# A weight stream whose two parts are made by the loads themselves: a rounding transfer and an adding one

## The chip, the cores and the metric

The kernel runs on one core of a Trainium2 chip. The metric is the device time of one execution in microseconds, the median of three runs; lower is better.

## The reference

Two layers of an encoder over 512 tokens of 1024 features, all in float32. Each layer projects the normed input, mixes it in three branches, merges them by gates, and adds a gated feed-forward part and an embedding part:

```python
for i in range(DEPTH):                       # DEPTH = 2
    z = rmsnorm(x, mix_norm[i]) @ w_in[i]    # 1024 x 6312
    u_rnn, u_gelu, c_q, ckv_rope, fq, fk, fv, f_logit, gate_logit = split_columns(z)
    y_a = rglru_branch(u_rnn, u_gelu, ...) @ w_br_a[i]
    y_b = mla_branch(c_q, ckv_rope, ...) @ w_br_b[i]
    y_c = fox_branch(fq, fk, fv, f_logit, fox_bf[i]) @ w_br_c[i]
    g = sigmoid(gate_logit + gate_b[i]).reshape(B, S, 3, D)
    x = x + (g[:, :, 0] * y_a + g[:, :, 1] * y_b + g[:, :, 2] * y_c) @ w_o[i]
    hf = rmsnorm(x, ffn_norm[i]) @ w_gate_up[i]
    x = x + (silu(hf[..., :D_FF]) * hf[..., D_FF:]) @ w_down[i]      # D_FF = 2816
    x = x + sigmoid(rmsnorm(x, ple_norm[i]) @ w_ple_gate[i]) * (p[i] @ w_ple[i])
return rmsnorm(x, final_norm)
```

What matters here is the number of weights: about 40 million float32 values, each used once for all 512 tokens.

## The kernel before

Activations lie feature by token, in pages of 128 features by 512 tokens. TensorE multiplies float32r values; to keep float32 accuracy, each operand X is held as two float32r parts, hi (X rounded) and lo (X minus hi), and each product is three matmuls, hi by hi, hi by lo and lo by hi (`mm3`). So each 128x128 weight tile costs three matmuls of 512 columns.

The weights come as one stream in the order of use (class `Stream`). A unit is four tiles side by side, 128 partitions by 512 columns, 256 KB; there are 606 of them (`NUNITS`). Before, a unit passes through two rings. `_load` (L99) brings it by a transfer on SP's queue into one of four pages of the tile `raw`. `_split` makes the two parts in one of five pages of `hl`, each of 512 columns of hi and 512 of lo: ScalarE casts raw into hi (L112), VectorE subtracts hi from raw into lo (L113). `_ensure`, called when the first tile of a unit is taken, records loads and splits ahead of the products, as far as the rings reach. The last 16 units (from `KEPT` on) get pages of the large pool `pr` in place of pages of `hl`, since they are used twice, each time for half the tokens. Four units (`PACKED`) have both parts side by side for a narrow product.

Other names that matter: `pf` and `pr` are pools of pages (float32, and float32r with both parts), `bank` the eight PSUM banks. L221, L218, L225 are VectorE helpers, L230 and L233 ScalarE helpers, L237 is every matmul. POOL issues small transfers beside its memsets: masks and rotary tables (L403, L404, L493), a row's copies for attention (L587, L592, L594, L937), the input of the residual (L1010), the embedding input (L1083), and x between the layers (L1113).

The order on each engine is set by a scheduler, which goes by data dependence and simulated readiness; what stands in `high_priority()` goes first among what is ready. Every engine then runs its own queue in order, and an instruction that waits for a semaphore holds back all that is behind it. POOL's transfers count on eight semaphores in turn (DMASW0 to DMASW7 in the orders below), so each also waits for the transfer issued eight before it.

Of the kernel before, what the change touches and what calls it, by code (L numbers as in the profile page):

```python
# [26 lines left out]
# columns of w_in  # L27
# [3 lines left out]
# columns of the small per-partition vectors, per layer  # L31
# [3 lines left out]
V_LAM = DEPTH * NV          # lambdas of all layers, side by side  # L35
# [3 lines left out]
NUNITS = 606                # units of four 128x128 weight tiles in the stream  # L39
KEPT = NUNITS - 16          # from here on the stream is kept on chip: it is used twice  # L40
PACKED = (8, 9, 311, 312)  # units whose tiles hold the parts of 64 columns side by side


class Pages:
    """Pages of one tile, handed out oldest-freed first."""
# [39 lines left out]
class Stream:  # L85
    """The weights, in the order in which TensorE uses them: loaded ahead, split into two
    float32r parts that sum to the float32 value."""

    def __init__(self, tc, wdram, raw, hl, nraw, nhl):
        self.tc, self.nc, self.wdram, self.raw, self.hl = tc, tc.nc, wdram, raw, hl  # L90
        self.nraw, self.nhl = nraw, nhl
        self.pos, self.spec = 0, []
        self.loaded, self.done = 0, 0
        self.pages, self.kept = None, {}

    def _load(self, u):
        s = (u % self.nraw) * 512
        c = 512 * (u % 2)
        self.nc.sync.dma_start(self.raw[:, s:s + 512], self.wdram[u // 2][:, c:c + 512])  # L99

    def _split(self, u):
        s = (u % self.nraw) * 512
        src = self.raw[:, s:s + 512]
# [7 lines left out]
        with self.tc.high_priority():  # L111
            self.nc.scalar.copy(hi, src)  # L112
            self.nc.vector.tensor_tensor(lo, src, hi.bitcast(F32), op=ALU.subtract)  # L113
# [8 lines left out]
    def _ensure(self, u):  # L122
        last = min(u + self.nhl - 1, NUNITS - 1)
        while self.loaded < min(self.nraw, NUNITS):
            self._load(self.loaded)
            self.loaded += 1
        while self.done <= last:
            self._split(self.done)
            self.done += 1
            while self.loaded < min(self.done + self.nraw, NUNITS):  # L130
                self._load(self.loaded)
                self.loaded += 1

    def tile(self, spec):
        """hi and lo of the next 128x128 tile"""
# [7 lines left out]
    def again(self, i):  # L143
        """tile i of the stream, one of those that were kept"""
# [7 lines left out]
    def wide(self, spec):  # L152
        """hi and lo of a 128x512 tile, at the start of a unit"""
# [13 lines left out]
class Trunk:  # L167
    def __init__(self, ctx, tc, wst, vec, xT, pT, trig, masks, outT, last):
# [7 lines left out]
        NR, NF, NRAW, NHL = 31, 20, 4, 5  # L176
# [26 lines left out]
    # -- small things ---------------------------------------------------------------------  # L203

    def cols(self, n):
        """n columns of a ring of small per-partition values"""
# [37 lines left out]
    # -- products, as generators that stop after every k tile -----------------------------  # L244

    def dense(self, spec, xs, evac, m=128):
        """out[m, tokens] = sum over k of W[k, m] * X[k, tokens]; xs are pages"""
# [11 lines left out]
    def group(self, specs, xs, evacs):  # L259
        """several of them side by side, k tile by k tile"""  # L260
# [20 lines left out]
    # -- RMSNorm ---------------------------------------------------------------------------  # L281

    def norm_add(self, st, x):
        """adds the squares of x (128 features) to the sums of norm st"""
# [17 lines left out]
    def norm_sum(self, st, n, fold=None):  # L302
        """token-major 1/rms, times fold, and its diagonal for the broadcast"""
# [10 lines left out]
        # 1/sqrt(v): a first value from the bits of v, good to 2e-3, and three Newton steps  # L314
# [30 lines left out]
    def normed(self, x, g):  # L345
        """page with both parts of x * g"""
# [5 lines left out]
    def after_norm(self, st, n, gen, s1, s2):  # L352
        """the first products after a norm, whose results wait for it; the sums are taken after
        s1 of their steps and the broadcast after s2"""
# [11 lines left out]
    # -- set-up -----------------------------------------------------------------------------  # L366

    def log1p_exp_neg(self, out, t1, t2, u, e):
        """out = log1p(s) / 2 with s = exp(-|u|), as atanh(y) with y = s / (2 + s)"""
# [11 lines left out]
    def setup(self):  # L381
# [6 lines left out]
        for k in range(KD):  # L388
            nc.sync.dma_start(self.x[k].ap, self.a_x[k])
            if k < 4:  # L390
                self.w._load(k)
        self.w.loaded = 4
        # TensorE's clock rises while it is busy
# [30 lines left out]
        # softplus(-lambda), times 2  # L424
# [9 lines left out]
    # -- mixers -------------------------------------------------------------------------------  # L434
# [4 lines left out]
    def mix(self, layer):  # L439
# [6 lines left out]
        # recurrent branch  # L446
# [39 lines left out]
        # rotary key and forget logits  # L486
# [12 lines left out]
        def rope(z, src, out_h, out_l, m):  # L499
            """z may be src"""  # L500
# [8 lines left out]
        def key_and_forget():  # L509
            """the rotary key, and the sums of the log forget gates; both parts of the weights side  # L510
            by side, so that one pass serves both"""
# [33 lines left out]
        # attention pieces  # L545
        qp, kp = {}, {}

        def ev_heads(pages, p, r, fox, is_q):
            """two heads' queries or keys to their pages, times 1/rms unless r is None"""
            f8 = 0.125 if fox and is_q else 1.0  # L550

            def f(b):
# [21 lines left out]
                for e in range(2):  # L574
# [3 lines left out]
                    if fox:  # L578
                        # queries [hi, hi | lo, extra], keys [hi, lo | hi, extra] or [lo, hi | hi, extra]
# [26 lines left out]
        def values(spec, X, rT):  # L606
            """token-major values: page per token tile, [head][hi 64 | lo 64]"""
# [23 lines left out]
        # recurrence: gates, then the scan  # L631
# [32 lines left out]
        def lru_tail():  # L664
            # one change of ScalarE's tables for all of them
# [724 lines left out]
```

## Time and profile before

| | |
|---|---|
| runs | 1825.26 us median (1824.38, 1825.26, 1826.84) |
| profiled execution, first to last instruction | 1825.0 us (no other time of it is given) |
| granted TensorE clock, mean | 0.996 |
| HBM read, written | 173.98 MB, 4.21 MB, 98 GB/s over the span |
| weight loads on SP's queue | 606 of 256 KB, 2.6 us from issue to landing |

In the rows below, a group of instructions reads: line, engine, operation, output<-inputs, count | busy us in total, mean ns of one | idle us of its engine just before them, and what ended most of that idle time. A row of waits reads: engine and line that waited <- what it waited for: us in total, times, longest. A row of the timeline reads: start us, duration us, engine, line, operation, count, and the idle time before it in brackets. A row of stretches reads: from:to, length, busy us of the asked instructions (their count), granted clock, share of the DMA engines busy, GB/s. A row of a DMA queue reads: packets, MB, share of 16 engines' span; one of DMA issues ends in KB and the median us from issue to landing.

### The profile page before, as it was taken

To read this page: it belongs to the slowest core of one execution; us is meant where nothing else is said; L and a number is where in the kernel's file an instruction comes from. 1 tells how busy PE (TensorE), PEld (TensorE's weight loads), DVE (VectorE), ACT (ScalarE), POOL (GpSimd) and SP (SyncE) were. 2 spreads that over 40 slices of the span, in tenths; PEclk is the share of its full clock that TensorE was granted. 3 is DMA by queue.
4 is the path that set the end of the run, shared out by engine and by line. 5 is a ranking of instruction groups with operands and counts; after the bars stand their busy time and mean duration, and the time that the engine had idled before them with its cause. 6 is when DMAs were issued, how large, how long until landed. Compare 5 with 4: busy or idle time off the path is not lost. (4 is left out here: it accounts for less than half of the span.)

```text
span 1825.0 us, 24155 instructions
## 1 busy us (share of the span) xinstructions
PE 1807.5 (99%) x8490; PEld 1505.6 (82%) x8490; DVE 1210.6 (66%) x2421; ACT 817.1 (45%) x1562; POOL 117.2 (6%) x234
## 2 busy tenths in 40 slices
PE   9999999999999999999999999999999999999998
PEld 8778888888888888888887788888888888888887
DVE  8997678866665555444778966888576555553457
ACT  4766556553333333223447655565533333332243
POOL 1220001100000000000103200010000000000000
PEclk9999999999999999999999999999999999999999
DMA  5232223324222222322333322242232222232231
GB/s 178 91 131 82 81 78 117 97 72 139 96 95 96 96 98 98 110 94 97 133 110 122 106 81 82 91 116 85 87 128 92 99 98 97 95 109 99 98 116 47
DMA packets 98826, 184.17 MB, mean 101 GB/s; under 512 B 13552, under 2 KB 14752, under 8 KB 98704
## 3 DMA queue, kind: packets, MB, share of 16 engines
q1 hardware_dynamic: 89280, 162.04, 25.7%
q0 software_dynamic: 8416, 19.45, 3.8%
q8 instruction: 66, 1.08, 0.2%
q10 hardware_dynamic: 1008, 1.14, 0.2%
q14 instruction: 56, 0.46, 0.1%
HBM read 173.98 MB, written 4.21 MB: 98 GB/s over the span
## 5 line engine op out<-in xcount | busy, mean ns | idle before, releaser
L237 PE MATMUL bank<-pr,hl 128*128 128x512 f32 (+1 forms) x6812 | 1602.9, 392 | 2.8 <-ACT pr L233 1.1
L237 PEld LDWEIGHTS bank<-pr,hl 128*128 128x128 f32 (+1 forms) x6812 | 1269.9, 188 | 267.3 <-ACT pr L233 2.0
L112 ACT CAST hl<-raw 128x512 fp32r<-128x512 f32 x590 | 364.3, 618 | 672.0 <-PE bank L237 403.8
L113 DVE TENSOR_TENSOR hl<-raw,hl 128x512 fp32r<-128x512 f32 x590 | 404.2, 686 | 378.6 <-ACT hl L112 360.4
L221 DVE TENSOR_TENSOR pf<-pf 128x512 f32<-128x512 f32 (+3 forms) x235 | 151.1, 651 | 31.8 <-ACT pf L230 29.9
L221 DVE TENSOR_TENSOR pf<-bank,pf 128x512 f32<-128x512 f32 (+3 forms) x198 | 132.8, 676 | 58.6 <-PE bank L237 32.1
L230 ACT ACTIVATE pf<-pf 128x512 f32<-128x512 f32 (+1 forms) x145 | 86.1, 600 | 112.7 <-DVE pf L221 110.5
L237 PE MATMUL bank<-pr 128*128 128x256 f32 (+5 forms) x704 | 120.7, 303 | 4.1 <-ACT pf L230 2.2
L237 PEld LDWEIGHTS bank<-pr 128*128 128x128 f32 (+1 forms) x704 | 102.7, 191 | 14.1 <-ACT pf L230 2.7
L221 DVE TENSOR_TENSOR pr<-pf,pr 128x512 fp32r<-128x512 f32 (+2 forms) x126 | 85.6, 682 | 4.5 <-ACT pr L233 3.5
L230 ACT ACTIVATE pf<-bank,small 128x384 f32<-128x384 f32 (+3 forms) x130 | 68.9, 531 | 38.5 <-DVE small L836 35.4
L233 ACT CAST pr<-pf 128x512 fp32r<-128x512 f32 (+1 forms) x114 | 70.4, 620 | 33.2 <-DVE pf L218 23.1
L853 ACT CAST pth<-bank 128x128 fp32r<-128x128 f32 (+3 forms) x128 | 54.0, 427 | 58.7 <-PE bank L828 50.5
L221 DVE TENSOR_TENSOR ptl<-bank,pth 128x128 fp32r<-128x128 f32 (+3 forms) x128 | 61.7, 485 | 13.9 <-ACT pth L853 9.9
L836 DVE TENSOR_REDUCE small<-bank 128x1 f32<-128x384 f32 (+3 forms) x128 | 61.6, 484 | 7.6 <-PE bank L237 6.5
L237 PE MATMUL bank<-hl,pr 128*128 128x512 f32 x240 | 56.3, 391 | 0.4 <-DVE hl L113 0.4
L828 PE MATMUL bank<-identr,pf 128*128 128x128 f32 x320 | 55.0, 273 | 0.0
L237 PEld LDWEIGHTS bank<-hl,pr 128*128 128x128 f32 x240 | 44.7, 188 | 10.3 <-DVE hl L113 1.1
L225 DVE TENSOR_SCALAR pf<-pf,small 128x384 f32<-128x384 f32 (+3 forms) x128 | 48.6, 383 | 2.6
L828 PEld LDWEIGHTS bank<-identr,pf 128*128 128x128 f32 x320 | 40.2, 140 | 8.3
L218 DVE SCALAR_TENSOR_TENSOR pf<-pf,bank 128x512 f32<-128x512 f32 x48 | 32.6, 683 | 21.6 <-PE bank L237 21.2
L230 ACT ACTIVATE pf<-bank,vec 128x512 f32<-128x512 f32 x60 | 40.9, 689 | 12.9 <-PE bank L237 12.5
(112 smaller groups left out, 796.6 us busy)
## 6 DMA issues: line engine op xcount, KB each, us to landing
raw<-wst SPq DMA_DIRECT2D x606, 256.0 KB, 2.6
pf<-xT POOLq DMA_DIRECT2D x16, 256.0 KB, 3.3
pr<-pr POOLq DMA_DIRECT2D x32, 128.0 KB, 2.6
pf<-xs POOLq DMA_DIRECT2D x16, 256.0 KB, 3.2
pf<-trig POOLq DMA_DIRECT2D x12, 256.0 KB, 3.1
pf<-xT SPq DMA_DIRECT2D x8, 256.0 KB, 5.3
xs<-pf POOLq DMA_DIRECT2D x8, 256.0 KB, 2.7
pf<-pT POOLq DMA_DIRECT2D x4, 256.0 KB, 3.1
```

Source lines behind the costliest of these rows:

```text
L112: self.nc.scalar.copy(hi, src)
L113: self.nc.vector.tensor_tensor(lo, src, hi.bitcast(F32), op=ALU.subtract)
L218: self.nc.vector.scalar_tensor_tensor(out, a, s, b, op0=op0, op1=op1)
L221: self.nc.vector.tensor_tensor(out, a, b, op=op)
L225: self.nc.vector.tensor_scalar(out, a, s1, None, op0=op0)
L230: return self.nc.scalar.activation(out, a, f, **kw)
L233: self.nc.scalar.copy(hi, src)
L237: self.nc.tensor.matmul(out, a, b, start=start, stop=stop, skip_group_check=True)
L828: nc.tensor.transpose(T[:, c], p2.ap[:, c], self.ident[:, :])
L836: nc.vector.reduce_max(R[t][:, 0:1], S[:, :m], axis=AX.X, negate=True)
L853: self.nc.scalar.copy(hi, src)
```

## The change

`raw` is no longer used for weights. For each unit POOL issues a transfer from HBM into hi that casts float32 to float32r; ScalarE writes the negative of hi into lo; POOL issues a second transfer of the same 256 KB from HBM that adds the weights onto lo. VectorE takes no part. `_load` and `_split` become one function, `hl` has six pages where it had five, and `raw` has two where it had four (its later use as scratch pages, near the end, has two as well). Comments are taken out elsewhere, which moves the line numbers: L112 and L113 have their counterparts in L109 (rounding transfer), L110 (negation) and L111 (adding transfer); L237 becomes L228, L221 L212, L230 L221, L233 L224, L493 L481, L1083 L1071.

```diff
     def _load(self, u):
-        s = (u % self.nraw) * 512
         c = 512 * (u % 2)
-        self.nc.sync.dma_start(self.raw[:, s:s + 512], self.wdram[u // 2][:, c:c + 512])
-
-    def _split(self, u):
-        s = (u % self.nraw) * 512
-        src = self.raw[:, s:s + 512]
+        src = self.wdram[u // 2][:, c:c + 512]
         if u >= KEPT:
             self.kept[u] = self.pages.take()
         hi, lo = self._parts(u)
...
         with self.tc.high_priority():
-            self.nc.scalar.copy(hi, src)
-            self.nc.vector.tensor_tensor(lo, src, hi.bitcast(F32), op=ALU.subtract)
+            self.nc.gpsimd.dma_start(hi, src)
+            self.nc.scalar.activation(lo, hi.bitcast(F32), AF.Copy, scale=-1.0)
+            self.nc.gpsimd.dma_start(lo, src, accum_op=ALU.add)
...
     def _ensure(self, u):
-        last = min(u + self.nhl - 1, NUNITS - 1)
-        while self.loaded < min(self.nraw, NUNITS):
+        while self.loaded <= min(u + self.nhl - 1, NUNITS - 1):
             self._load(self.loaded)
             self.loaded += 1
-        while self.done <= last:
-            self._split(self.done)
-            self.done += 1
-            while self.loaded < min(self.done + self.nraw, NUNITS):
-                self._load(self.loaded)
-                self.loaded += 1
...
-        NR, NF, NRAW, NHL = 31, 20, 4, 5
+        NR, NF, NRAW, NHL = 31, 20, 2, 6
...
         for k in range(KD):
             nc.sync.dma_start(self.x[k].ap, self.a_x[k])
-            if k < 4:
-                self.w._load(k)
-        self.w.loaded = 4
...
-        self.tmp = Pages(self.raw, 4, 512, "late float32")
+        self.tmp = Pages(self.raw, 2, 512, "late float32")
```

Three places of the program show how the instructions stand. A row is line, operation, output<-input and size, and in brackets the engines' or transfers' semaphores that it waits for.

POOL at the start, before: after its constants it issues the mask loads and clears five pages, and then waits for its copies.

```order
L398 MEMSET eps 128x1
L399 MEMSET eps 128x1
masks.py:197 MEMSET pf 128x128
L403 DMA fmask<-masks 128x128
L404 DMA pf<-masks 32x128
L585 MEMSET pr 4x512 [waits Pool_49]
```

POOL at the start, now:

```order
L109 DMA hl<-wst 128x512 x6
L386 MEMSET eps 128x1
L387 MEMSET eps 128x1
masks.py:197 MEMSET pf 128x128
L391 DMA fmask<-masks 128x128
L392 DMA pf<-masks 32x128
L573 MEMSET pr 4x512 [waits Pool_49]
L573 MEMSET pr 4x512 x4
L111 DMA hl<-wst 128x512 [waits DMASW0_49,Activation_49]
L481 DMA pf<-trig 128x512 [waits DMASW1_49,DMAHW2_49,DVE_49,Activation_49]
L111 DMA hl<-wst 128x512 [waits DMASW2_49,Activation_49]
```

Six rounding transfers now stand ahead of all of it, and the first adding transfer behind it.

POOL in the feed-forward part of the first layer, the long dense stretch, before: between the residual's input and the next layer's preparation it has two loads.

```order
L1010 DMA pf<-xT 128x512 [waits DMASW2_49,DVE_49]
L1010 DMA pf<-xT 128x512 [waits DMASW3_49,DVE_49]
L1083 DMA pf<-pT 128x512 [waits DMASW4_49,DVE_49]
L1083 DMA pf<-pT 128x512 [waits DMASW5_49,DVE_49]
L585 MEMSET pr 4x512 [waits PE_49]
```

POOL at the end of the same stretch, now:

```order
L109 DMA hl<-wst 128x512 [waits DMASW7_49,PE_49]
L111 DMA hl<-wst 128x512 [waits DMASW0_49,Activation_49]
L1071 DMA pf<-pT 128x512 [waits DMASW1_49,DVE_49]
L109 DMA hl<-wst 128x512 [waits DMASW2_49,PE_49]
L111 DMA hl<-wst 128x512 [waits DMASW3_49,Activation_49]
L109 DMA hl<-wst 128x512 [waits DMASW4_49,PE_49]
```

Casts and adds alternate; in most of the stream (468 of 606 units) the add of a unit stands behind the cast of the next unit, and ahead of that of the one after. A cast waits for TensorE to free its page, an add for ScalarE's negation.

ScalarE in the same stretch, before and now:

```order
L112 CAST hl<-raw 128x512 [waits DMAHW5_49,PE_49,Activation_49]
L230 ACTIVATE pf<-pf 128x512 [waits DVE_49]
L112 CAST hl<-raw 128x512 [waits DMAHW6_49,PE_49,Activation_49]
L112 CAST hl<-raw 128x512 [waits DMAHW7_49,PE_49,Activation_49]
L112 CAST hl<-raw 128x512 [waits DMAHW0_49,PE_49,Activation_49]
L233 CAST pr<-pf 128x512 [waits DVE_49]
```

```order
L110 ACTIVATE hl<-hl 128x512 [waits DMASW3_49,DMASW2_49,PE_49]
L221 ACTIVATE pf<-pf 128x512 [waits DVE_49,Activation_49]
L110 ACTIVATE hl<-hl 128x512 [waits DMASW5_49,DMASW4_49,PE_49]
L110 ACTIVATE hl<-hl 128x512 [waits DMASW7_49,DMASW6_49,PE_49]
L110 ACTIVATE hl<-hl 128x512 [waits DMASW1_49,DMASW0_49,PE_49]
L224 CAST pr<-pf 128x512 [waits DVE_49]
```

The negation stands where the cast stood, and waits for a rounding transfer in place of a load into raw. At the very end of POOL's queue 15 adds stand together behind the last casts.

More of the change, by code (lines that the diff above doesn't have):

```diff
@@ L92, in __init__ @@
         self.pos, self.spec = 0, []
-        self.loaded, self.done = 0, 0
+        self.loaded = 0
         self.pages, self.kept = None, {}
     def _load(self, u):
-        s = (u % self.nraw) * 512
         c = 512 * (u % 2)
-        self.nc.sync.dma_start(self.raw[:, s:s + 512], self.wdram[u // 2][:, c:c + 512])
-    def _split(self, u):
-        s = (u % self.nraw) * 512
-        src = self.raw[:, s:s + 512]
+        src = self.wdram[u // 2][:, c:c + 512]
         if u >= KEPT:
```

## Prediction

> **What bounds the kernel now.** I read the head of the page first, then its groups by line, the chain that ended last, the waits, and last the stretches and the timeline of the long dense part.
>
> ```profile
> span 1825.0 us, 24155 instructions
> PE 1807.5 (99%) x8490; PEld 1505.6 (82%) x8490; DVE 1210.6 (66%) x2421; ACT 817.1 (45%) x1562; POOL 117.2 (6%) x234
> ```
> ```profile
> 1315.18 482.91 PE bank L237 x2267
> ```
> ```profile
> L112 ACT CAST hl<-raw 128x512 fp32r<-128x512 f32 x590 | 364.3, 618 | 672.0 <-PE bank L237 403.8
> L113 DVE TENSOR_TENSOR hl<-raw,hl 128x512 fp32r<-128x512 f32 x590 | 404.2, 686 | 378.6 <-ACT hl L112 360.4
> ```
> ```profile
> ACT hl L112 <- PE bank L237: 403.8, 238, 3.5
> ...
> ACT hl L112 <- DMA raw<-wst: 11.4, 13, 2.3
> ```
>
> TensorE has 17.5 us without work in 1825.0, and one piece of the chain runs 483 us on matmuls alone. The two instructions that make the parts of a weight, the cast on ScalarE (L112) and the subtraction on VectorE (L113), are not late: the cast sits idle 404 us because TensorE has not yet let go of a page of hl, and only 11 us because a load had not landed. So preparation runs ahead of use everywhere, and TensorE is the bound. A busy TensorE can hide pipelining, but the next rows show its pace directly.
>
> ```profile
> 802.18 0.62 ACT L112 CAST hl<-raw 128x512 fp32r<-128x512 f32 x1 [2.10 <-PE bank L237]
> 802.84 0.69 DVE L113 TENSOR_TENSOR hl<-raw,hl 128x512 fp32r<-128x512 f32 x1 [2.03 <-ACT hl L112]
> 804.90 0.62 ACT L112 CAST hl<-raw 128x512 fp32r<-128x512 f32 x1 [2.10 <-PE bank L237]
> ```
> ```profile
> 22.00:130.00 108.00, 22.03 (x36) 0.97 0.34 113
> 130.00:365.00 235.00, 42.24 (x68) 1.00 0.28 90
> 365.00:413.00 48.00, 7.40 (x12) 1.00 0.21 73
> 413.00:866.00 453.00, 102.68 (x166) 1.00 0.30 102
> 866.00:933.00 67.00, 14.47 (x24) 1.00 0.38 134
> 933.00:1030.00 97.00, 20.87 (x34) 1.00 0.33 110
> 1030.00:1263.00 233.00, 41.62 (x67) 1.00 0.29 92
> 1263.00:1310.00 47.00, 7.41 (x12) 1.00 0.21 71
> 1310.00:1750.00 440.00, 100.03 (x162) 1.00 0.30 103
> ```
>
> The first rows are the steady rhythm: one unit (four 128x128 weight tiles, twelve matmuls) each 2.72 us, released by TensorE. The second set counts the casts of L112 in each stretch. The four attention stretches (130 to 413 and 1030 to 1310) use 159 units in 563 us, 3.54 us each, since other matmuls stand between. The five dense ones use 422 units in 1165 us, 2.76 us each. Whatever makes the parts of a unit in less than that costs nothing; whatever takes longer is paid 422 times.
>
> **The change, part by part.** Taken away: 606 subtractions of 0.686 us, 416 us of VectorE, and 606 loads from SP's queue. The gain of both is nothing: the cover is TensorE itself, and the whole of its idle time (17.5 us, 7 of them before the first product) is the most that could come back. On ScalarE the cast of 0.62 us becomes a negation of the same size; the nearest row is an activation from SBUF to SBUF at 0.63 us, so this also is nothing by itself:
>
> ```profile
> L230 ACT ACTIVATE pf<-pf 128x512 f32<-128x512 f32 x126 | 79.1, 631 | 106.1 <-DVE pf L221 104.0 <-DMA pf<-xT 1.3
> ```
>
> What it waits for changes: no longer a load made early into raw, but a cast that can only start when TensorE frees a page of hl.
>
> Added: two transfers of 256 KB for each unit, both issued by POOL. POOL's own time is small: a 256 KB issue takes 0.54 us, so 1212 of them are 654 us beside 117, under half the span.
>
> ```profile
> L1010 POOL DMA_DIRECT2D pf<-xs x8: 536/537/766, 1310.5 to 1340.3; - x8
> ```
> ```profile
> q0 software_dynamic: 8416, 19.45, 3.8%
> ```
> ```profile
> q1 hardware_dynamic: 23784, 43.30, 27.6%
> q0 software_dynamic: 800, 2.62, 2.0%
> ```
> ```profile
> raw<-wst SPq DMA_DIRECT2D x606, 256.0 KB, 2.6
> ...
> pr<-pr POOLq DMA_DIRECT2D x32, 128.0 KB, 2.6
> pf<-xs POOLq DMA_DIRECT2D x16, 256.0 KB, 3.2
> ```
>
> Two prices matter, the time that a transfer holds the 16 DMA engines and its time to landing. Plain loads on SP's queue hold them 0.75 us for 256 KB (27.6% of the 453 us from 413 to 866, by 166 units). On POOL's queue it is 0.91 us there (2.0% of 453 us for 2.62 MB, of which 0.262 is one unit) and 0.93 over the whole span (3.8% of 1825 us for 19.45 MB, 4.2 MB of it the pr<-pr copies, which are float32r on both sides). So a copy from POOL with another type costs about a plain one; I take **0.95 us** for the rounding transfer, 3.2 us to landing.
>
> The adding transfer has no row. Below: it costs one pass like the others, 0.95 us. Above: its engines do nothing else from issue to landing, 3.2 us. I take **1.9 us**, two passes, because an add fetches two operands of 256 KB, the weights and the negative, where a copy fetches one; the low end is nearer in kind, and I go up by that one pass only. The Trainium skill, "Collectives: The Full Stack", section on the bandwidth ceiling and the fold count, gives 62.28 GB/s for a gather, which copies, and 32.35 for a reduce-scatter, which adds, and puts the difference down to the second source read. No trace here shows it. By that ratio of 1.93 the add would hold the engines 1.83 us, an estimate from that page, and the sum below would end near 2003 us.
>
> Now the order on POOL in the dense part: the cast of unit u+1, the add of unit u, the cast of u+2, the add of u+1. An add cannot be issued before its cast has landed and ScalarE has negated it, and the cast two units on stands behind that add. So from add to add two units on: issue 0.54, landing 3.2, negation 0.63, and two hops of 0.05 (802.84 less 802.18 and 0.62 is 0.04): 4.47 us. ScalarE is busy 45% of the time, half an instruction of 0.62 on average then stands ahead: 0.14. And the cast's data queue behind the add just issued in the same queue: 1.9 less the 0.54 of head start, 1.36. Together 5.97 us for two units, **2.99 us a unit**. The DMA engines by themselves: 0.95, 1.9, and 0.1 for the rest of POOL's queue (69 us over 606 units), **2.95 us a unit**. Both are over 2.76, so the supply becomes the bound, if only just. Two limits this close and an engine load of 98% will leave gaps; I take 5% more, 3.15 us.
>
> The dense part: 422 units by (3.15 less 2.76), **165 us**. Attention at 3.54 has room on average, but POOL there also carries its memsets and small copies of 0.5 us, which wait on VectorE and TensorE with the weights now queued behind them; I take 0.15 us for 159 units, **24 us**.
>
> The start:
>
> ```profile
> 1.32 0.68 POOL L403 DMA_DIRECT2D fmask<-masks  x1 [0.33 <-issue]
> 2.00 0.53 POOL L404 DMA_DIRECT2D pf<-masks  x1
> ...
> 3.51 2.74 POOL L585 MEMSET pr<- 4x512 f32 x5
> ...
> 5.95 0.67 DVE L113 TENSOR_TENSOR hl<-raw,hl 128x512 fp32r<-128x512 f32 x1
> ...
> 7.08 15.23 PE L237 MATMUL bank<-pr,hl 128*128 128x512 f32 x56
> ...
> 12.49 0.57 POOL L493 DMA_DIRECT2D pf<-trig  x1 [2.23 <-ACT pf L230]
> ```
>
> Six casts (3.2 us), two mask loads (1.2) and five memsets (2.7) stand before the first add, which is so issued near 8 us and lands near 11, where the second part of unit 0 was there at 6.6 and TensorE asked for it about 2 us after 7.1. The third add stands behind the second trig load, which waited for its page until 12.5. I take **5 us**. At the end:
>
> ```profile
> 1764.47 5.92 PE L237 MATMUL bank<-pr 128*128 128x256 f32 x48
> ```
>
> The last 16 units are used at half width, 12 matmuls in 1.48 us, and their adds stand together behind the last casts: 16 by 1.9 is 30 us against 24. I take **6 us**.
>
> Sum, against the profiled execution's 1825.0: 1825 + 165 + 24 + 5 + 6 = **2025 us**. That span is 0.26 below the median of the runs (1825.26), so no correction is needed.
>
> **Rivals.** First, *the add costs one pass*. The loop is then 4.47 + 0.41 + 0.14, 2.51 us a unit, and the engines' sum 2.0; TensorE still bounds, and only start and end are paid: 1832, or up to 1880 if single waits on POOL are not covered. For it: the casts' rows show no price beyond a copy. The point at which it flips is an add of 1.44 us (two units in 5.51).
>
> Second, *not slower*: the same cheap add, and in addition TensorE finds enough first-part products at the start to wait for nothing: 1822 to 1829. It decides only where the first add lands by about 9 us, when TensorE has used up the products of unit 0 that need no second part; the start's order, which puts 16 POOL instructions ahead of that add, speaks against it.
>
> Third, *a heavy add*, which holds the engines for 3.2 us. 4.25 us a unit: 422 by 1.49 is 629, attention 159 by 0.71 is 113, ends 20: 2587 us. For it: nothing in the trace says that engines read, add and write back at copying speed.
>
> Fourth, *VectorE holds up POOL*. Its tensor_scalar instructions are quicker than others of the size (0.48 us for 512 columns, where L113 takes 0.69); minimum, median and maximum in ns stand behind the counts:
>
> ```profile
> L225 DVE TENSOR_SCALAR pf<-pf,small x128: 268/378/489, 128.1 to 1308.4; 128x128 f32<-128x128 f32 x32, 128x256 f32<-128x256 f32 x32, 128x384 f32<-128x384 f32 x32, 128x512 f32<-128x512 f32 x32
> L225 DVE TENSOR_SCALAR pr<-pf,vec x48: 468/482/602, 4.2 to 1756.2; 128x512 fp32r<-128x512 f32 x48
> L225 DVE TENSOR_SCALAR pr<-identr,small x42: 278/282/293, 31.4 to 1802.2; 128x128 fp32r<-128x128 f32 x42
> ...
> L225 DVE TENSOR_SCALAR pr<-pf x16: 416/416/428, 435.7 to 1352.9; 128x512 fp32r<-128x512 f32 x16
> ```
>
> If each of these 234 (by 0.4 us) delayed one transfer that is due, 94 us, with the ends 1930. The Trainium skill, "SBUF — State Buffer", in its box on VectorE blocking DMAs, says that such an instruction shuts GpSimd out of writing descriptors for its whole length. The trace hardly agrees: the longest of those eight issues was 0.77 us against 0.54.
>
> If the rounding transfer did not round, the second part would be zero; that changes results, and no time.
>
> **How the numbers follow.** The forecast (supply bound by some tenths of a us, 1880 to 2300) gets 0.46; the one-pass add with losses 0.18; not slower 0.06; the heavy add (2300 to 3100) 0.26; VectorE's lock 0.04. The range runs from 1832, the hidden case, to 2600, the heavy case at the landing bound. A change under 0.2% (3.6 us) is what a measurement could not tell from none. Faster has 0.02, same 0.04, both out of the second rival, slower 0.94.
>
> **What would show it.** Right: TensorE idle for some 0.4 us each unit in 413 to 866, the wait naming hl, its releaser a transfer from wst; the spacing of L110 near 3.15 us; DMA share above 0.8 in the dense part. An add's landing time near 4.5 us supports two passes; near 3.2 and an unchanged spacing, the first rival; a DMA share near 1 with spacing over 4, the third. POOL issues far longer than 0.54 us would speak for the fourth, or for a dearer making of descriptors, which I have priced at nothing: that, and a slower rounding, would make the prediction wrong upward.

## The result and the profile after

| | before | changed |
|---|---|---|
| median of 4 runs, on the same chip | 1825.49 us | 2058.75 us (2053.34 to 2060.65) |
| profiled execution, first to last instruction | 1825.0 us | 2058.9 us (its own time 2060.65) |
| granted TensorE clock, mean | 0.996 | 0.985 |

The change makes the kernel slower by 12.7%: the ratio is 1.1273, interval 1.1257 to 1.1289. The forecast was 2025 us. The weights still arrive in the same order and the same matmuls are issued, 8490 of them; what is new is that TensorE waits for its weights. The head of the page of the changed kernel, its groups (as before: busy and mean ns, then the idle time of the engine just before, and its releaser) and its transfers:

```profile
span 2058.9 us, 24216 instructions
PE 1903.6 (92%) x8490; PEld 1500.0 (73%) x8490; DVE 835.2 (41%) x1815; ACT 810.3 (39%) x1562; POOL 973.5 (47%) x1446
...
q0 software_dynamic: 186016, 336.19, 78.9%
...
L111 POOL DMA_DIRECT2D hl<-wst x590 | 526.1, 897 | 921.9 <-ACT hl L110 830.9
L110 ACT ACTIVATE hl<-hl 128x512 fp32r<-128x512 f32 x590 | 370.9, 630 | 1069.6 <-DMA hl<-wst 1014.7
L109 POOL DMA_DIRECT2D hl<-wst x590 | 482.5, 839 | 80.0 <-PE bank L228 72.6
...
hl<-wst POOLq DMA_DIRECT2D x1172, 256.0 KB, 4.5
```

Three waits form a ring. ScalarE's negation (L110) waits 1015 us for the rounding transfer to land. POOL's adding transfer (L111) waits 831 us for that negation. The next rounding transfer (L109), which stands right behind the add in POOL's queue, waits only 73 us for TensorE to free a page, so the pages are mostly free before it can use them. Before the change it was the other way round: the cast waited 404 us for TensorE and 11 us for loads. VectorE, relieved of 606 subtractions, has fallen from 66 to 41% busy, and nothing came of it. The waits of TensorE itself (both of its queues), on the new transfers:

```profile
PEld bank L228 <- DMA hl<-wst: 211.9, 259, 5.4
PE bank L228 <- DMA hl<-wst: 109.0, 161, 4.6
```

Now the pace in the two long dense stretches. The first two rows are of the kernel before (casts of L112), the other two of the changed one (negations of L110); columns are from:to, length, busy us (count), clock, share of the DMA engines, GB/s.

```profile
440.00:840.00 400.00, 90.37 (x146) 1.00 0.29 100
1340.00:1740.00 400.00, 90.97 (x147) 1.00 0.29 100
```
```profile
480.00:980.00 500.00, 99.84 (x158) 0.99 0.82 169
1540.00:1960.00 420.00, 84.70 (x134) 1.00 0.82 169
```

Before, 293 units in 800 us: 2.73 us each. Now 292 in 920 us: **3.15 us each**, the number forecast. The two long stretches hold 328 units (166 and 162), so they lost 328 by 0.42, 138 us, of the 234. TensorE's busy time in the two windows,

```profile
480.00:980.00 500.00, 461.55 (x1897) 348.48 (x1895) 128.06 (x213) 136.65 (x227) 224.15 (x322) 0.99 0.82 169
1540.00:1960.00 420.00, 390.21 (x1602) 291.93 (x1603) 101.90 (x170) 115.36 (x191) 188.63 (x269) 1.00 0.82 169
```

(first column after the length), leaves 68 us idle, 0.23 us a unit. The other half of the 0.42 us is inside what the view counts as busy: a matmul takes 0.243 us there on average (851.75 by 3499) where it took 0.226 before (400.00 us by 1770, from 440 to 840), 0.21 us for the twelve of a unit. The ends of matmuls are modelled in this view, so it cannot say where inside a matmul the time goes; but TensorE waits for more than the idle time shows.

The ring itself in the timeline of the changed kernel, steady part:

```profile
605.85 0.85 POOL L111 DMA_DIRECT2D hl<-wst  x1 [2.54 <-ACT hl L110]
606.39 0.86 POOL L109 DMA_DIRECT2D hl<-wst  x1
607.47 0.63 ACT L110 ACTIVATE hl<-hl 128x512 fp32r<-128x512 f32 x1 [1.92 <-DMA hl<-wst]
608.40 0.84 POOL L111 DMA_DIRECT2D hl<-wst  x1 [1.14 <-ACT hl L110]
608.94 0.86 POOL L109 DMA_DIRECT2D hl<-wst  x1
610.68 0.63 ACT L110 ACTIVATE hl<-hl 128x512 fp32r<-128x512 f32 x1 [2.06 <-DMA hl<-wst]
611.61 0.85 POOL L111 DMA_DIRECT2D hl<-wst  x1 [1.80 <-ACT hl L110]
```

An add is issued at 605.85, and 0.54 later the cast behind it (606.39); the row of an issue lasts 0.85 us here, yet the next one starts before it ends. That cast's data let the negation begin at 610.68, the second negation from there, and its add goes out 0.93 later, at 611.61. From add to the add two units on it is 5.76 us here. Over the whole span the cast's landing has a median of 4.7 us:

```profile
L109 POOL DMA_DIRECT2D hl<-wst x590: 527/862/1546, 1.2 to 1988.4; - x197
...
DMA to landing us min/median/max: 2.7/4.7/9.8
```

That gives 0.54 + 4.7 + 0.93 = 6.17 us for two units, 3.09 us each. These are typical values, and the spacing is a mean: followed unit by unit through the two long stretches, a cast's issue to its negation takes 4.88 us on average, the negation to its add 0.97, the add to the cast two units on 0.47. Together they are 6.32 us, 3.16 a unit, which is the whole spacing.

Outside the long stretches. The last cast of a transposed page in each layer's attention is a mark that both kernels have; the first two rows are of before, the other two of the changed kernel:

```profile
416.89 0.59 ACT L853 CAST pth<-bank 128x512 fp32r<-128x512 f32 x1
1315.28 0.59 ACT L853 CAST pth<-bank 128x512 fp32r<-128x512 f32 x1
```
```profile
456.08 0.58 ACT L841 CAST pth<-bank 128x512 fp32r<-128x512 f32 x1 [0.41 <-PE bank L816]
1470.83 0.57 ACT L841 CAST pth<-bank 128x512 fp32r<-128x512 f32 x1
```

The start and first mixer lost 39 us; the stretch from there through the first feed-forward part to the end of the second attention 116 us; the rest, the second feed-forward part and the end, 78 us. And the start:

```profile
8.68 0.59 POOL L111 DMA_DIRECT2D hl<-wst  x1
...
15.44 4.38 PE L228 MATMUL bank<-pr,hl 128*128 128x512 f32 x12 [4.64 <-DMA hl<-wst]
```

The first add goes out at 8.68 us, and TensorE stands still 4.64 us for weights; the forecast took 5.

### The profile page after: what moved, and what is told of

The parts are those of the page before. It is cut to its first block, busy times and chain, and to the rows that moved or that the text cites. A ratio compares the mean times of both kernels' runs of the same rounds, so it can differ in the third digit from the quotient of the medians.

```text
span 2058.9 us, 24216 instructions
## 1 busy us (share of the span) xinstructions
PE 1903.6 (92%) x8490; PEld 1500.0 (73%) x8490; DVE 835.2 (41%) x1815; ACT 810.3 (39%) x1562; POOL 973.5 (47%) x1446
## 3 DMA queue, kind: packets, MB, share of 16 engines
q1 hardware_dynamic: 2016, 3.15, 0.5%
## 4 chain that ended last, share of the span: by engine, by line
issue 34%; PE 26%; POOL 24%; DMA 10%; DVE 4%; ACT 2%; POOLq 0%; DVEq 0%; ACTq 0%
PE bank L228 25%; POOL hl L109 14%; POOL hl L111 9%; DMA hl<-wst 8%; DVE pf L209 1%; DMA pr<-wst 1%; ACT pf L221 1%; DVE pr L212 1%; PE bank L816 1%; ACT hl L110 1%; DVE pf L212 0%; DVE pf L663 0%; DVE pr L209 0%; POOL pf L998 0%; DMA pr<-pr 0%
## 5 line engine op out<-in xcount | busy, mean ns | idle before, releaser
L228 PE MATMUL bank<-pr,hl 128*128 128x512 f32 (+1 forms) x6812 | 1689.2, 400 | 111.1 <-DMA hl<-wst 98.5
L228 PEld LDWEIGHTS bank<-pr,hl 128*128 128x128 f32 (+1 forms) x6812 | 1259.0, 190 | 464.2 <-DMA hl<-wst 198.5
L111 POOL DMA_DIRECT2D hl<-wst x590 | 526.1, 897 | 921.9 <-ACT hl L110 830.9
L110 ACT ACTIVATE hl<-hl 128x512 fp32r<-128x512 f32 x590 | 370.9, 630 | 1069.6 <-DMA hl<-wst 1014.7
L109 POOL DMA_DIRECT2D hl<-wst x590 | 482.5, 839 | 80.0 <-PE bank L228 72.6
L212 DVE TENSOR_TENSOR pf<-bank,pf 128x512 f32<-128x512 f32 (+3 forms) x198 | 132.6, 674 | 287.3 <-PE bank L228 166.1
L212 DVE TENSOR_TENSOR pf<-pf 128x512 f32<-128x512 f32 (+3 forms) x235 | 152.2, 654 | 213.8 <-ACT pf L221 210.8
L212 DVE TENSOR_TENSOR pr<-pf,pr 128x512 fp32r<-128x512 f32 (+3 forms) x126 | 85.7, 687 | 336.6 <-ACT pr L224 327.6
L228 PE MATMUL bank<-pr 128*128 128x256 f32 (+4 forms) x704 | 121.3, 302 | 8.1 <-ACT pf L221 6.5
L228 PEld LDWEIGHTS bank<-pr 128*128 128x128 f32 (+1 forms) x704 | 104.7, 191 | 21.8 <-ACT pf L221 7.5
L212 DVE TENSOR_TENSOR ptl<-bank,pth 128x256 fp32r<-128x256 f32 (+3 forms) x128 | 61.8, 485 | 94.9 <-ACT pth L841 91.5
L221 ACT ACTIVATE pf<-pf 128x512 f32<-128x512 f32 (+1 forms) x145 | 84.3, 591 | 15.6 <-DVE pf L212 12.0
L221 ACT ACTIVATE pf<-bank,small 128x128 f32<-128x128 f32 (+3 forms) x130 | 68.3, 526 | 46.1 <-DVE small L824 43.1
L224 ACT CAST pr<-pf 128x512 fp32r<-128x512 f32 (+2 forms) x114 | 69.2, 612 | 22.7 <-DVE pf L209 14.8
L228 PE MATMUL bank<-hl,pr 128*128 128x512 f32 x240 | 61.8, 411 | 10.6 <-DMA hl<-wst 10.5
L228 PEld LDWEIGHTS bank<-hl,pr 128*128 128x128 f32 x240 | 46.7, 197 | 24.3 <-DMA hl<-wst 13.4
L824 DVE TENSOR_REDUCE small<-bank 128x1 f32<-128x128 f32 (+3 forms) x128 | 62.0, 486 | 4.2 <-PE bank L228 2.4
L841 ACT CAST pth<-bank 128x256 fp32r<-128x256 f32 (+3 forms) x128 | 52.9, 422 | 14.9 <-PE bank L816 9.1
```

The costliest lines, as they stand in the source:

```text
L109: self.nc.gpsimd.dma_start(hi, src)
L110: self.nc.scalar.activation(lo, hi.bitcast(F32), AF.Copy, scale=-1.0)
L111: self.nc.gpsimd.dma_start(lo, src, accum_op=ALU.add)
L212: self.nc.vector.tensor_tensor(out, a, b, op=op)
L221: return self.nc.scalar.activation(out, a, f, **kw)
L228: self.nc.tensor.matmul(out, a, b, start=start, stop=stop, skip_group_check=True)
```

## The experiments

The theory (A) was that the ring sets the pace: issue, landing, negation and the next issue, in order on one queue, with two units under way in each turn. Its rivals were that the DMA engines are full (B: cast 0.95 and add 1.9 us each unit), and that an add costs no more than a copy, or that POOL or VectorE is in the way. The edits are shown against the changed kernel where nothing else is said.

### Distance on the queue: two casts ahead, and none

The first kernel holds each unit's negation and add back until the cast of the unit two further on has been issued. Three units are then under way in one turn of the ring; the transfers and their number stay the same.

```diff
-            self.nc.gpsimd.dma_start(hi, src)
-            self.nc.scalar.activation(lo, hi.bitcast(F32), AF.Copy, scale=-1.0)
-            self.nc.gpsimd.dma_start(lo, src, accum_op=ALU.add)
+            c = self.nc.gpsimd.dma_start(hi, src)
+        self.held.append((hi, lo, src))
+        if len(self.held) > 2 or u == NUNITS - 1:
+            ...
+                hi, lo, src = self.held.pop(0)
+                with self.tc.high_priority(), self.tc.issue_after(c.ins):
+                    self.nc.scalar.activation(lo, hi.bitcast(F32), AF.Copy, scale=-1.0)
+                    self.nc.gpsimd.dma_start(lo, src, accum_op=ALU.add)
```

> The add of a unit is issued behind the cast two units on (it was one unit on); nothing else is changed. Theory A, a round trip bounds (issue 0.54, cast to landing 4.7, negation to issue 0.93 are 6.2 us, shared by two units in the changed kernel): three units now share it, 2.1 us a unit, so TensorE's 2.73 bounds the dense part again, spacing of the negations near 2.75 there, and the time comes to 1850 to 1900 us. Theory B, the 16 DMA engines bound (their share of 0.82 is all they give): spacing stays at 3.1 to 3.2 and the time at 2030 to 2060 us.

Measured: 1866.14 us, ratio 1.0217 (1.0200 to 1.0234). Its stretches (negations, L117) and the first of its waits:

```profile
460.00:860.00 400.00, 92.97 (x147) 1.00 0.99 198
1380.00:1780.00 400.00, 93.91 (x149) 1.00 0.98 197
```
```profile
POOL hl L110 <- PE bank L235: 660.4, 476, 4.1
...
POOL hl L118 <- ACT hl L117: 78.0, 72, 4.0
```

296 units in 800 us, 2.70 us each: TensorE's own pace is back, and 193 of the 233 us with it. The waits have changed places: the cast now waits 660 us for TensorE to free a page (73 in the changed kernel), and the add 78 us for the negation (831 there). The same transfers are issued in another order, so B, as the forecast summed it (2.95 us a unit), cannot be a limit. The 43 us that this kernel is still longer than the one before (profiled executions) lie, by the marks used above, in the three segments with 19, 18 and 5 us.

The opposite: the cast of a unit is put behind the add of the one before, so that one unit is under way in each turn.

```diff
-        with self.tc.high_priority():
+        with self.tc.high_priority(), ExitStack() as after:
+            if self.last is not None:
+                after.enter_context(self.tc.issue_after(self.last.ins))
...
-            self.nc.gpsimd.dma_start(lo, src, accum_op=ALU.add)
+            self.last = self.nc.gpsimd.dma_start(lo, src, accum_op=ALU.add)
```

> The cast of a unit is issued behind the add of the unit before it, so that one unit has the round trip to itself. Theory A: 5 to 5.5 us a unit (the cast lands sooner, since little else is under way): 422 dense units by 2.5 and 159 by 1.7 are 1300 us more than the kernel before, near 3150 us. Theory B: the engines' load is the same, so the time stays within some per cent of 2059 us.

Measured: 3619.27 us, ratio 1.9820 (1.9780 to 1.9859). A stretch (negations, L113), and one turn of the ring in the timeline:

```profile
760.00:1560.00 800.00, 86.53 (x137) 0.84 0.44 92
```
```profile
1005.25 0.86 POOL L114 DMA_DIRECT2D hl<-wst  x1 [4.63 <-ACT hl L113]
1005.80 0.86 POOL L112 DMA_DIRECT2D hl<-wst  x1
1010.18 0.63 ACT L113 ACTIVATE hl<-hl 128x512 fp32r<-128x512 f32 x1 [5.23 <-DMA hl<-wst]
1011.11 0.86 POOL L114 DMA_DIRECT2D hl<-wst  x1 [4.46 <-ACT hl L113]
```

5.84 us a unit. Add to cast 0.55, cast to negation 4.38, negation to next add 0.93: 5.86, the whole period. The direction is the theory's; the size was missed upward (some 3150 us was expected, at 5 to 5.5 us a unit). In part that is the cast's landing, which those 5 to 5.5 us put at 3.5 to 4 and which is 4.4 even here: 0.6 us for each of 581 units is some 340 of the 470 us. The rest was not traced. With the changed kernel in between, distances of 0, 1 and 2 casts give 5.84, 3.15 and 2.70 us a unit: one turn of about 6 us, divided by one, by two, and by three until TensorE is slower than that.

### The price of the add

The adding transfer is issued as a plain cast of the same size.

```diff
-            self.nc.gpsimd.dma_start(lo, src, accum_op=ALU.add)
+            self.nc.gpsimd.dma_start(lo, src)
```

> The second transfer of each unit writes the weights over the negative instead of adding them (the same bytes from HBM, the same cast, the same waits and order), so the second parts are not what they should be; only the time is of use. If an add costs a second pass of 0.9 us on the engines, which stands ahead of the next cast: the cast lands about 1 us sooner, the round trip is 5.2 us for two units, the dense spacing 2.75, DMA share 0.6 to 0.65, time 1850 to 1900 us. If an add costs no more than a copy and the second transfer of any kind is what queues: spacing 3.1 to 3.2, time within 1% of 2059 us.

Measured: 1845.14 us, ratio 1.0105 (1.0090 to 1.0120). Its stretches (L110), its casts' transfers, and the issues of its second transfers (ns, minimum, median, maximum):

```profile
440.00:840.00 400.00, 92.95 (x147) 1.00 0.72 197
1360.00:1760.00 400.00, 94.21 (x149) 1.00 0.72 198
```
```profile
hl<-wst POOLq DMA_DIRECT2D x1172, 256.0 KB, 3.3
```
```profile
L111 POOL DMA_DIRECT2D hl<-wst x590: 527/528/762, 8.5 to 1783.8; - x197
```

The order on POOL is unchanged, and yet TensorE's pace is back, since both transfers land in 3.3 us: the turn is 0.54 + 3.3 + 0.93, 4.77 us for two units, 2.39 each, under TensorE's 2.70. So the distance costs only together with the longer landing beside adds. Whether a cast lands later because it queues behind the add, as the forecast had it, or because the two run side by side, was not separated. The time is 5 us under the range expected of a dearer add, and the share is 0.72 where 0.6 to 0.65 was expected. The shares also give prices, in time of the engines' packets: 0.72 by 2.70 us is 1.94 for two casts, **0.97 us** each. In the kernel with two casts ahead 0.985 by 2.70 is 2.66, which leaves **1.69 us** for an add; in the changed kernel 0.82 by 3.15 leaves 1.61. The kernel without adds is also the case in which the first rival would have held: it asked 1832 to 1880 us of an add at one pass.

Is there a second limit at all behind the ring? The kernel with two casts ahead showed a DMA share of 0.99. If that is a full load, a third transfer for each unit must be paid in full. So one is added to that kernel (and the edit is shown against it): a cast of the same weights into lo, which the negation then overwrites.

```diff
             c = self.nc.gpsimd.dma_start(hi, src)
+            c = self.nc.gpsimd.dma_start(lo, src)
```

> The kernel lag2 with a third transfer of 256 KB for each unit: the weights are cast into lo too, where the negation then overwrites them. Nothing else changes; it doubles the cast's load on the DMA engines. Their share in lag2's dense stretches is 0.985, 2.66 us a unit. If that share is the load they can carry: 2.66 and 0.97 make 3.6 us a unit, the dense spacing is 3.5 to 3.7, the time 2200 to 2300 us. If the share holds waiting that more transfers would fill: a spacing of 2.75 to 3.2 and a time below 2080 us.

Measured: 2044.84 us, ratio 1.1200 (1.1184 to 1.1217). Its stretches (negations, L118) and its queue over the whole span:

```profile
500.00:900.00 400.00, 83.94 (x134) 1.00 1.11 268
1500.00:1900.00 400.00, 84.49 (x135) 1.00 1.12 267
```
```profile
q0 software_dynamic: 274816, 494.57, 102.8%
```

269 units in 800 us, 2.97 us each, as expected if the share is no measure of a limit: each unit has one and a half times the transfers, they pass at 268 GB/s where two casts ahead had 198, and the share went to 1.11, which no full engine could show. By the prices above two casts and an add would need 3.63 us. So the share must add up packets' times that overlap, and 0.82 (or 0.99) of it was no sign that the engines were full. The prices are not fixed either: 1.11 by 2.97 is 3.30 us, less than their sum. They say what the view counts, and not how long a transfer keeps others out. What holds this kernel at 2.97 was not separated. Its landings are longer (5.4 to 6.1 us at the median), and its casts wait 378 us in all for TensorE to free a page, so the six pages may bound it as well as the turn.

### Each half alone

The rounding transfer alone: the weights also come by SP into raw as before, and VectorE subtracts. Then the adding transfer alone: ScalarE casts raw into hi and negates it, and POOL adds. In both, the rings are those of before (four pages of raw, five of hl). The edits are shown against the kernel before; d is the unit's place in HBM.

```diff
-            self.nc.scalar.copy(hi, src)
...
+            self.nc.gpsimd.dma_start(hi, d)
             self.nc.vector.tensor_tensor(lo, src, hi.bitcast(F32), op=ALU.subtract)
```
```diff
             self.nc.scalar.copy(hi, src)
-            self.nc.vector.tensor_tensor(lo, src, hi.bitcast(F32), op=ALU.subtract)
...
+            self.nc.scalar.activation(lo, hi.bitcast(F32), AF.Copy, scale=-1.0)
+            self.nc.gpsimd.dma_start(lo, d, accum_op=ALU.add)
```

> Half of the change alone: the rounded part comes by POOL's cast from HBM, the weights come also into raw by SP's queue, and VectorE subtracts as before; no negation, no add, rings as before (four pages of raw, five of hl). Theory A: no instruction of POOL waits for a landing, a cast has four units (11 us) to land and be subtracted, so 1825 to 1840 us. Theory B, two transfers a unit load the engines: 0.75 and 0.95 us are 1.7 of 2.76 us, also hidden, the same time. A rounding that is slow in itself (over 2 us a unit) would show as a dense spacing over 2.75 and a time above 1900 us.

> The other half alone: the weights come into raw by SP's queue and ScalarE casts them into hi as before; ScalarE then writes the negative into lo and POOL's adding transfer brings the same weights from HBM a second time; no subtraction on VectorE, no rounding transfer, rings as before (five pages of hl). If the round trip through the cast's landing is what costs (theory A), it is gone: an add needs 1.3 us on ScalarE after TensorE frees the page and lands within 4.5 of the 11 us that four units take, so the dense part stays at 2.73 us a unit and the time at 1825 to 1850 us. If the adds cost by themselves (theory B), the dense spacing is over 2.8 us and the time above 1900.

Measured: 1849.53 us (1.0133, 1.0116 to 1.0149) and 1852.41 us (1.0149, 1.0132 to 1.0166). The first is 10 us over its expectation, the second just over its upper end. The dense part keeps its pace in both; the first row is of the rounding transfer alone (subtractions, L116), the second of the adding one alone (negations, L116):

```profile
460.00:860.00 400.00, 101.67 (x147) 1.00 0.67 195
```
```profile
440.00:840.00 400.00, 93.38 (x148) 1.00 0.92 198
```

They are 2.72 and 2.70 us a unit, the second at a DMA share of 0.92. So neither half costs the dense part anything; it is the chain of a cast and an add through one queue that does, 233 us against some 25 for each half. Where these 25 go was looked at by the marks only: 14, 10 and 3 us in the three segments of the first kernel, 8, 5 and 11 in the second. What makes them was not tried.

### The remainder: mixers, start, other transfers

By the order, in 34 units, 31 of them in the mixers, the add stands ahead of the next cast, which is distance 0. This kernel makes the distance at least one, with the same held list (`> 1` in place of `> 2`).

> The changed kernel, with one rule more: the add of a unit is issued behind the cast of the next unit at least. In the change 34 units break that, 31 of them in the two mixers (their add stands ahead of the next cast), and for each of them one round trip serves a single unit, up to 2.9 us more. If that is why the mixers grew by 77 us: the end of the first attention part falls from 456 us to 420 to 436, and the time to 1980 to 2020 us (this order also gives 48 units of the last dense stretch the longer distance, which saves some 15 us of that). If the mixers' loss has another cause: 2040 to 2059 us.

Measured: 2004.67 us (1998.51 to 2013.13), ratio 1.0996 (1.0965 to 1.1027). Its stretches (L117) and its marks:

```profile
460.00:900.00 440.00, 89.12 (x141) 1.00 0.84 173
1480.00:1900.00 420.00, 85.36 (x135) 1.00 0.84 171
```
```profile
440.61 0.57 ACT L848 CAST pth<-bank 128x512 fp32r<-128x512 f32 x1
...
1420.79 0.57 ACT L848 CAST pth<-bank 128x512 fp32r<-128x512 f32 x1
```

The pace of the dense part is nearly that of the changed kernel (860 by 276, 3.12). The first segment takes 440.6 us (456.1 in the changed kernel), the second 980.2 (1014.7): 50 us back, about 5 of them from the 0.03 us in 166 units, the rest from the mixers. The time is inside the expected range, and the first mark just above it (436 at most was expected). In the changed kernel 32 of the 34 units stand between 208 and 476 us and between 1223 and 1492 us, in and just behind the two attention parts, so the loss fell there. Another 12 us come back in the last segment, where this order also has 48 units at distance two.

Five other transfers of POOL's queue (the tables, three of x, the embedding input; 256 KB each) go to SP's queue in three further kernels: with the change alone, with two casts ahead, and with two casts ahead and the first six units made the old way.

```diff
-                nc.gpsimd.dma_start(trig[i].ap, self.a_trig[i])
+                nc.sync.dma_start(trig[i].ap, self.a_trig[i])
```

(and so for four others)

> The changed kernel with the same five transfers moved to SP's queue; casts and adds in the order that the change has (an add one cast behind). Theory A: the round trip still bounds wherever units follow closely, and the moved transfers only take their waits out of the mixers: 2035 to 2055 us against 2059. If POOL's queue, not the round trip, was what made the mixers 77 us longer: below 2010 us.

> The kernel lag2 with its other large plain transfers (rotary tables, x for the second norm, x for the residual, the embedding input, x between the layers: L488, L688, L1005, L1078, L1108 there) moved from POOL's queue to SP's. If what lag2 still loses in the mixers (some 18 us in each layer) comes from weights standing behind those transfers on POOL, or the reverse: 1840 to 1855 us. If it comes from ScalarE's order (work for attention behind negations that wait for casts) or from TensorE's clock after a gap: within 5 us of lag2's 1866.

> The kernel lag2_sp, and the first six units made the old way: loaded by SP's queue into pages of pf, cast on ScalarE, subtracted on VectorE. If the start costs what the first products wait for there (TensorE idle 4.8 us from 10.4 to 15.2, and slower products after it): 6 to 10 us less than lag2_sp. If later waits take the time up again: the same as lag2_sp within 3 us.

Measured: 2077.97 us (1.1381, 1.1364 to 1.1398), 1858.71 (1.0184, 1.0168 to 1.0199) and 1856.43 (1.0177, 1.0158 to 1.0195). The first was expected faster than the change and is 19 us slower: moving other instructions let the scheduler lay the stream out anew, with 42 units at distance 0 in place of 34. That is a reading of the order, in line with the kernel before it, and not a separate proof. With two casts ahead the same move gives 7 us, between the two expectations. The start, where TensorE stood 5.46 us for weights at 16 us, loses that hole in the third kernel and the time moves by 2 us, less than the intervals tell apart; so what is saved there is presumably waited for later. No version is faster than the kernel before.

## Why the forecast was right, and where its terms were off

- *What bounds*: TensorE, with preparation running ahead. Shown: wherever the supply takes under 2.70 us a unit (two casts ahead, no add, either half), TensorE's pace returns, and what VectorE was spared brings nothing.
- *The ring of 5.97 us for two units*: right, and shown three ways, by its parts in the timeline, by distances 0, 1 and 2, and by its shortening without adds. Measured 6.17 (6.32 as a mean), with the landing of a cast at 4.7 where 3.2 + 1.36 were summed, and 0.93 from the negation's start to the add's issue where 0.87 were summed from landing to issue.
- *The 5% for two close limits*: the sum came out at 3.15, the number measured, by luck. The second limit, the engines' sum of 2.95, does not exist at that place: the same transfers pass at 2.70 with two casts ahead. The forecast had read the DMA share as a load that cannot pass 1, and it went to 1.11. What filled the step from 2.99 to 3.15 was the ring itself, whose parts make 3.16 as means.
- *The price of the add*: 1.9 us was taken, 1.6 to 1.7 measured by the shares, of a cast 0.97 (0.95 taken). The 0.95 was right without a row for it: the 256 KB transfers behind it have float32 on both sides in the kernel, so none of them was the copy to another type that the forecast took them for. What matters for the ring is another number, how much later a cast lands with an add ahead: 4.3 us against 3.3 at the median where one unit is under way, 4.7 in the changed kernel, so 1.0 to 1.4. The forecast's 1.36 is at the top of that. The Trainium skill, "Collectives: The Full Stack", section on the bandwidth ceiling and the fold count, has a ratio of 1.93 between a gather, which copies, and a reduce-scatter, which adds, in a ring of cores, for the second source read. By the shares 1.69 by 0.97 is 1.74 here, the same direction and a smaller step.
- *The dense part, +165 us*: 422 units by the 0.42 measured in 328 of them would be 177, 12 more than forecast.
- *Attention, +24, start 5, end 6*: what is left of 234 is 57 us, 22 more than the 35 forecast. The term that was too small is the 0.15 us for each of 159 units: the forecast saw the small copies on POOL, and took the order of the adds as it is in most of the stream. The 34 units whose add stands ahead of the next cast were left out of the sum, and the kernel with a distance of at least one gives some 45 us back in the first two segments. The hole of the start is there (4.64 us), but filling one like it brought next to nothing. In the kernel before, TensorE's 17.5 idle us are not 7 before the first product either: until 7.08 it runs 28 matmuls on ones and is idle for 1.05 us. That changes no term.
- *The rivals*. The one-pass add fell: a real one gives 1845 us, the add in the change 2059. The heavy add asked 4.25 us a unit and 2587 us; it fell with 3.15 and 2059, and with 2.70 at two casts ahead. Not slower fell. VectorE's hold on POOL does not show: the issues without adds have a median of 528 ns and a maximum of 762, at most 0.23 us more, where that rival needed some 0.4 us each time. The Trainium skill, "SBUF — State Buffer", box on VectorE blocking DMAs, would have the issues held for the length of an instruction; no such length appears among these 590 issues. The other way round there is something: the longest of VectorE's 128 tensor_scalar instructions that write pf from pf and small took 0.49 us before and take 0.80 in the changed kernel. Why was not tried.
- *The signs named*: spacing 3.15 (right), DMA share above 0.8 (right, 0.82, but not for the reason given), an add's landing near 4.5 (4.4), waits naming hl and wst (right). TensorE idle some 0.4 us a unit: 0.23 as idle time, the rest as longer matmuls. POOL issues far longer than 0.54 us were named as a sign for VectorE's hold or for dearer descriptors, and they are there: the issues of casts have a median of 0.86 us. They are not that rival's: without adds the median is 0.53. And they cost little by themselves, since the next issue still starts 0.54 us after the last.

## What to carry to other kernels

When a step of the work is a transfer, then an engine, then a second transfer, and both transfers stand in one in-order queue, the pace cannot be better than the round trip divided by the number of items that the order lets be under way between the two. Count that number in the order, and compare the result with the consumer's period, before adding up how busy the engines are. Here moving the second transfer one place further back in the queue was worth 193 us, and the 416 us of VectorE that the change removed was worth nothing, since VectorE did not bound. Look for the exceptions too: a kernel that puts 34 units of 606 in order got some 45 us back, more than the 35 that the forecast had for attention, start and end together. Two queues for the two transfers were not tried.

## What was not expected of the hardware

- The DMA share of the view goes over 1: 1.11 in the long stretches with three transfers a unit, at 268 GB/s. So a share of 0.99 (two casts ahead) does not show that the engines are full.
- A transfer that adds of 256 KB lands in 4.0 to 5.1 us at the median, in the kernels with two transfers a unit, where a casting one with no adds about takes 3.3, and takes 1.6 to 1.7 us of engine share against 0.97. At the end of the changed kernel's queue adds stand one behind the other, and go out 1.24 to 1.34 us apart:

```profile
2002.21 0.85 POOL L111 DMA_DIRECT2D hl<-wst  x1 [0.41 <-ACT pf L1081]
2003.45 0.85 POOL L111 DMA_DIRECT2D pr<-wst  x1 [0.40 <-issue]
2004.74 0.85 POOL L111 DMA_DIRECT2D pr<-wst  x1 [0.44 <-issue]
2006.08 0.85 POOL L111 DMA_DIRECT2D pr<-wst  x1 [0.48 <-DMA hl<-wst]
```

- With one unit under way, TensorE works 65% of the stretch (518 of 800 us) and its granted clock is 0.84 there, where it is 1.00 at full work. In that kernel the supply bounds, and the parts of the turn already make up the whole spacing (5.86 against 5.84 us). Whether such holes cost more in a kernel that is bound by TensorE now and then was not tried.
